# A hybrid decoder layer on one core: one head's attention put behind the next head's K/V quad, an operand block in another slot, two row vectors sent through DRAM, and the meta products raised in rank

## The chip, the core and the metric

The kernel runs on one core of a Trainium2 chip. Its time is the device time of one execution, in microseconds, from the first instruction to the last and what little lies around them; a comparison is made between medians of several runs. The engines are PE (matmuls, with its own weight loads, PEld), DVE (elementwise work and reductions), ACT (copies, casts, activations), POOL (elementwise work) and SP, which here only issues DMAs. Each engine works through its own list of instructions in order and waits on semaphores for the others.

## What is computed

One layer over 2048 tokens of width 1024, with 16 learned meta tokens ahead of them:

```python
hn = rms_norm(h, norm_g)                        # h = meta tokens, then x
proj = hn @ w_in                                # 1024 x 4096
cx, cb, cc, cg, q, k, v, rg = split(proj, 8)    # 512 columns each
conv_out = cb * conv3(cc * cx) * silu(cg)       # causal, three taps
qf, kf = rotary(q) * 128 ** -0.5, rotary(k)     # 4 heads of 128
ret = head_group_norm(retention(qf, kf, v)) * silu(rg)
y = rms_norm(h + concat(conv_out, ret) @ w_out, final_g)   # tokens of x alone
```

`retention` works in chunks of 128 tokens: inside a chunk the masked and decayed scores q k^T times v; across chunks a 128x128 state per head, which decays from chunk to chunk and takes up k^T v. The meta tokens give the first state and the first two columns of the convolution's history. All of it is in float32.

## The kernel before

**Products.** Every float32 operand of a large product is cast to a high part on ACT (L99, L102), and the rest is taken as a low part by a subtraction on DVE (L100, which calls L111, or L103). A product of two such operands is three matmuls: low x high, high x low, high x high. The work is cut in *quads*: a 2x2 arrangement of weight blocks (128 columns each, K over 4 tiles of 128) times a 2x2 arrangement of moving blocks (512 tokens each). `quad` (L199) does a quad as seven block products instead of eight, with sums and differences of the blocks as operands: 7 products x 4 K tiles x 3 matmuls = 84 matmuls of 128x512 at L208, product 0 to product 6, each against one moving operand m[0] to m[6]. The weights' sums are made on POOL and split by `stationary` (L121), in a ring of three buffers (RING); the moving operands stay in SBUF for a whole round, each high and low part in a slot of its own (`operand`, L139). `quad_plain` (L247) does a quad in eight block products, 96 matmuls at L258, and needs only the plain blocks: m[0], m[1], m[5] and m[7]. m[7] is the block B12, which no seven-product quad uses; it has no slot of its own and lies in slot 4 (`B12`, L33). The plain quads are done first in a round, while the operands that are sums get ready.

**Rounds.** The tokens are done in two rounds of 1024, and the output projection follows as a third stage. In a round come four heads (for each a K/V quad and a Q/RG quad), then four groups of the convolution (two quads each). In round 0 both quads of head 0 are plain; in round 1 and in the output stage only the first quad is. The four sums of round 1 and of the output's weights are made ahead by `prepare` (L181) while an earlier round runs, stored in DRAM (`sums_x`, `sums_w`), and read back by `prepared` (L191) into buffers t of the ring `gen` (GEN = 16 buffers, which also holds x, w, k, v, q, gates and outputs). SUMS (L34) says which operand each stored sum is: sum 0 is m[3], sum 1 is m[2], sum 2 is m[4], sum 3 is m[6]. At the turns of the rounds sums 1 and 3 are split before the plain quad and sums 0 and 2 after it. Slot 3 holds the plain weights (PLAIN_W) until the plain quad is done.

**Attention.** `head` (L517) traces the K/V quad, the Q/RG quad, the loads of the next quad's weights (`ahead`, L713), and then its attention: transposes of k and v (L573, L578), state updates (L588 on PE, L591 on DVE), scores (L601), the masked scores pm (L603, DVE), scores times v and q times state (L611, L612), group norm (L617 to L628), a transpose back (L635), the gate (L636) and a store.

**Row factors.** The factor 1/rms of every token is needed along the free axis. For each 512 tokens `row_factors` (L340) loads x, squares and sums on ACT (L317), takes the power on POOL (L274) and spreads the 512 values over all partitions with `spread` (L277): a diagonal matrix on DVE (L281), a matmul with ones on PE (L288), a copy and a square on ACT (L291, L293). Those of round 0 come early in round 0, those of round 1 in its convolution groups.

**Meta products.** In round 0 `meta_products` (L386) multiplies the 16 meta tokens with each of the quad's four raw weight blocks (L392): 4 K tiles x 4 blocks, two instructions each, so 32 small matmuls a call and eight calls.

**The order of the work.** `schedule_with_timeline_sim=True` (L825): a planner walks through the program before the run and fixes the order of each engine's list. It simulates the engines with its own estimates of durations, and whenever an engine is free it gives it, of the instructions that are ready in its simulation, the one of best rank. The rank is the place in program order; inside `tc.high_priority(offset=n)` an instruction ranks as if it stood n places earlier.

Of the kernel before, what the change touches and what calls it, by code (L numbers as in the profile page):

```python
# [32 lines left out]
FIRST_W, PLAIN_W, B12 = 2, 3, 4  # L33
# [35 lines left out]
def hybrid_trunk(ctx: ExitStack, tc: tile.TileContext, t, out: bass.AP, chunk_decay):  # L69
# [75 lines left out]
    def parts(m, i, kt, src, factor=None):  # L145
        hi, lo = operand(i, kt)
# [172 lines left out]
    def spread_factors(ss, rr, rr2):  # L319
# [5 lines left out]
        spread(rc, P, rr, rr2)  # L325
# [14 lines left out]
    def row_factors(r, f):  # L340

        f.extend([row_tile("rr"), row_tile("rr2"), []])
        for j in range(2):
            ss = small.tile([P, 2, CH], F32, name="ss", tag="ss")
            for c in range(CH):
                row_squares(ss, r, j, c)
                yield
            f[2].append(spread_factors(ss, *(a[:, j * HB : (j + 1) * HB] for a in f[:2])))
        yield
# [36 lines left out]
    def meta_products(blocks):  # L386
# [3 lines left out]
        for kt in range(KH):  # L390
            for i in (3, 2, 1, 0):
                nc.tensor.matmul(  # L392
                    four[i], meta_s[:, i % 2 * KH + kt, :], blocks[i][:, kt * P : (kt + 1) * P],
                    start=kt == 0, stop=kt == KH - 1,
                )
# [121 lines left out]
    def head(h, r, m, rot_t, f, blocks, ahead, first=(), between=()):  # L517


        between = iter(between)  # L520
# [19 lines left out]
        next(between, lambda: None)()  # L540
        q, sg = [None, None], [None, None]
# [25 lines left out]
        blocks = ahead()  # L567
        states = [state[h]]
# [73 lines left out]
        return blocks  # L642

    def output(pair, m, final_g):
# [78 lines left out]
    for r in range(NR):  # L723
# [7 lines left out]
        if r == 0:  # L731
# [3 lines left out]
            def begin(half):  # L735
# [4 lines left out]
                load_x(r), gain_of, {(0, 0): lambda: begin(0), (0, KH - 1): lambda: begin(1), (0, KT - 1): normalise_meta}  # L740
# [26 lines left out]
        else:  # L767
# [61 lines left out]
```

## Time and profile before

| | |
|---|---|
| median of 3 runs | 900.6 us (899.18 to 901.88) |
| the profiled execution | 903.85 us, of which its span is 902.1 |
| matmuls at L208, three groups of 1008 | mean 390 to 397 ns each |
| matmuls at L258, three groups of 128 | mean 395 to 396 ns each |
| DVE, split of a weight (L111 wl<-ra) x216 | mean 892 ns |
| ACT, cast of a weight (L99) x216 | mean 620 ns |
| POOL, weight sums (L111 ra<-ra) x72 | mean 1570 ns |
| HBM | 90.92 MB read, 25.17 MB written |

A row of a timeline reads: start in us from the span's start, length in us, engine, line, operation, out<-in, sizes, and in brackets how long the engine had stood idle before it and which instruction ended that. Matmuls overlap each other, so the pace of PE is read from the starts, not from the lengths. L12 is line 12 of the kernel before. A row of waits reads: who, for whom, us in total, times, longest.

### The profile page before, as it was taken

The page shows a single profiled execution, that of the slowest core. Times are in us where ns is not written, and L with a number is a line of the kernel's source. Part 1 is how long each engine was busy: PE and PEld are TensorE (multiplying, and loading weights), DVE is VectorE, ACT ScalarE, POOL GpSimd, SP SyncE. Part 2 cuts the span into 40 slices and gives each one's busy share as a digit, 9 for nine tenths or more (in the row PEclk, how much of TensorE's full clock was granted, in tenths as well). Part 3 has the DMA queues.
Part 4 walks back from the last instruction along what each step waited for, and adds up shares of the span by engine and source line. Part 5 has one row for each costly group of instructions (what it writes and reads, how often), then busy time and mean ns, then how long its engine had stood idle before and what let it go on. Part 6 is the DMA issues. An engine that isn't in the chain of part 4 may idle for free.

```text
span 902.1 us, 12862 instructions
## 1 busy us (share of the span) xinstructions
PE 885.0 (98%) x4407; PEld 727.8 (81%) x4407; DVE 714.6 (79%) x1173; ACT 406.1 (45%) x815; POOL 398.9 (44%) x294
## 2 busy tenths in 40 slices
PE   8998999999999999999999999999999999999996
PEld 5787888888878777788888888888888878788885
DVE  6798888897686776899889899777667697866764
ACT  8771342424344443655333332433333465554553
POOL 0533132323355554461333323345546445777763
PEclk9998999999999999999999999999999999999999
DMA  9711352623234232744125262113231685555532
GB/s 333 239 40 38 104 195 59 205 82 107 79 103 127 78 108 78 253 180 141 38 73 203 73 236 68 50 56 90 57 88 48 210 280 178 162 186 152 182 111 93
DMA packets 76242, 116.94 MB, mean 130 GB/s; under 512 B 7632, under 2 KB 24336, under 8 KB 76176
## 3 DMA queue, kind: packets, MB, share of 16 engines
q1 hardware_dynamic: 76176, 116.11, 40.1%
q8 instruction: 35, 0.57, 0.3%
q14 instruction: 31, 0.25, 0.1%
HBM read 90.92 MB, written 25.17 MB: 129 GB/s over the span
## 4 chain that ended last, share of the span: by engine, by line
PE 83%; DVE 9%; DMA 3%; ACT 2%; issue 2%; POOL 1%; SPq 0%; POOLq 0%; DVEq 0%; ACTq 0%
PE pj L208 66%; PE pj L258 7%; DVE ml L111 2%; DVE wl L111 2%; PE ms L611 2%; PE ms L612 1%; PE ms L601 1%; PE ms L588 1%; PE ms L392 1%; DVE rot L513 1%; DMA ra<-in_w_in 1%; PE ms L635 1%; PE ms L573 1%; DVE rot L512 1%; PE ms L578 1%
## 5 line engine op out<-in xcount | busy, mean ns | idle before, releaser
L208 PE MATMUL pj<-mh,wl 128*128 128x512 f32 x1008 | 400.0, 397 | 1.0 <-ACT tc L215 0.8
L208 PE MATMUL pj<-ml,wh 128*128 128x512 f32 x1008 | 394.2, 391 | 1.1 <-DVE ml L111 1.1
L208 PE MATMUL pj<-mh,wh 128*128 128x512 f32 x1008 | 393.4, 390 | 0.0
L99 ACT CAST wh<-ra 128x512 fp32r<-128x512 f32 x216 | 133.8, 620 | 315.1 <-PE pj L208 272.4
L208 PEld LDWEIGHTS pj<-mh,wl 128*128 128x128 f32 x1008 | 189.6, 188 | 43.1 <-ACT tc L215 2.2
L208 PEld LDWEIGHTS pj<-ml,wh 128*128 128x128 f32 x1008 | 189.8, 188 | 39.6 <-DVE ml L111 1.9
L208 PEld LDWEIGHTS pj<-mh,wh 128*128 128x128 f32 x1008 | 189.6, 188 | 39.8
L111 DVE TENSOR_TENSOR wl<-ra,wh 128x512 fp32r<-128x512 f32 x216 | 192.4, 892 | 36.2 <-ACT wh L99 35.2
L111 POOL TENSOR_TENSOR ra<-ra 128x512 f32<-128x512 f32 x72 | 113.0, 1570 | 82.0 <-DVE qg L556 32.3
L108 POOL TENSOR_TENSOR sa<-ra 128x512 f32<-128x512 f32 x36 | 54.9, 1525 | 122.6 <-DVE wl L111 62.1
L111 POOL TENSOR_TENSOR ra<-sa,ra 128x512 f32<-128x512 f32 x36 | 52.2, 1450 | 98.3 <-DVE wl L111 98.0
L215 ACT COPY tc<-pj 128x512 f32<-128x512 f32 x108 | 62.6, 580 | 0.0
L258 PE MATMUL pj<-ml,mh 128*128 128x512 f32 x128 | 50.8, 396 | 0.1
L258 PE MATMUL pj<-mh,mh 128*128 128x512 f32 x128 | 50.2, 395 | 0.0
L258 PE MATMUL pj<-mh,ml 128*128 128x512 f32 x128 | 48.5, 396 | 1.5 <-DVE ml L111 1.5
L624 POOL TENSOR_TENSOR rp<-rs,neg_half 128x4 f32<-128x4 f32 x16 | 19.9, 1245 | 51.0 <-DVE rs L108 50.8
L466 POOL TENSOR_TENSOR c<-c,rr 128x512 f32<-128x512 f32 x16 | 30.0, 1874 | 24.0 <-DVE c L454 13.6
L108 DVE TENSOR_TENSOR tc<-pj,tc 128x512 f32<-128x512 f32 x32 | 22.0, 688 | 23.4 <-PE pj L208 23.4
L111 DVE TENSOR_TENSOR ml<-t,mh 128x512 fp32r<-128x512 f32 x40 | 36.6, 961 | 0.8 <-ACT mh L99 0.8
L99 ACT CAST wh<-sa 128x512 fp32r<-128x512 f32 x36 | 22.3, 620 | 32.7 <-PE pj L208 32.7
L665 DVE TENSOR_TENSOR yo<-pj,yo 128x512 f32<-128x512 f32 x32 | 22.0, 688 | 18.8 <-POOL yo L108 8.9
L466 POOL TENSOR_TENSOR c<-c,tc 128x512 f32<-128x512 f32 x16 | 27.3, 1706 | 19.0 <-ACT tc L492 17.6
(128 smaller groups left out, 1134.3 us busy)
## 6 DMA issues: line engine op xcount, KB each, us to landing
ra<-in_w_in SPq DMA_DIRECT2D x128, 256.0 KB, 2.7
x<-in_xT SPq DMA_DIRECT2D x48, 256.0 KB, 5.1
w<-in_w_out SPq DMA_DIRECT2D x32, 256.0 KB, 5.0
ra<-mixed SPq DMA_DIRECT2D x32, 256.0 KB, 2.7
yo<-in_x SPq DMA_DIRECT2D x32, 256.0 KB, 4.4
ra<-in_x SPq DMA_DIRECT2D x16, 256.0 KB, 3.7
mixed<-qg SPq DMA_DIRECT2D x16, 256.0 KB, 2.3
sums_x<-x SPq DMA_DIRECT2D x16, 256.0 KB, 2.4
```

Source lines behind the costliest of these rows:

```text
L99: nc.scalar.copy(out=hi, in_=src)
L108: eng.tensor_tensor(out=out, in0=a, in1=b, op=ALU.add)
L111: eng.tensor_tensor(out=out, in0=a, in1=b, op=ALU.subtract)
L208: nc.tensor.matmul(bank, a[:, ks], b, start=first and kt == 0 and n == 0, stop=kt == KH - 1 and n == 2, skip_group_check=not first,)
L215: nc.scalar.copy(out=c, in_=bank)
L258: nc.tensor.matmul(banks[i], a[:, ks], b, start=half + kt + n == 0, stop=half == 1 and kt == KH - 1 and n == 2,)
L392: nc.tensor.matmul(four[i], meta_s[:, i % 2 * KH + kt, :], blocks[i][:, kt * P : (kt + 1) * P], start=kt == 0, stop=kt == KH - 1,)
L466: eng.tensor_tensor(out=out, in0=a, in1=b, op=ALU.mult)
L512: nc.vector.tensor_tensor(out=rot[:h, :w], in0=a[h:], in1=table[h:, 1, :], op=ALU.mult)
L611: nc.tensor.matmul(o[:, cs], pm[:, cs], vt[j][:, cs], start=True, stop=False)
L624: nc.gpsimd.tensor_tensor(out=rp, in0=rs, in1=neg_half.rearrange("p (c a) -> p c a", a=1), op=ALU.pow)
L665: last[0] = nc.vector.tensor_tensor(out=y, in0=pp, in1=y, op=ALU.add)
```

## The change

Four edits. (1) `head` becomes a generator of three parts: K/V quad, Q/RG quad and loads, attention. In round 0 the attention of head 0 is traced after the K/V quad of head 1; all other heads keep their order. (2) B12 takes slot 4 only in round 0; in round 1 and the output stage it takes slot 6, so that sums 1 and 2 (m[2], m[4]) are split before the plain quad and sums 0 and 3 (m[3], m[6]) after it; sum 0 is loaded before it. (3) The row factors of round 1 are written to DRAM and read back with one row going to all partitions; the square is then taken from SBUF. (4) The matmuls of `meta_products` rank 400 places earlier (HIGH).

```diff
-FIRST_W, PLAIN_W, B12 = 2, 3, 4
+FIRST_W, PLAIN_W = 2, 3
...
-    def operand(i, kt):
-        slot = B12 if i == 7 else i
+    def operand(i, kt, slot=None):
+        slot = i if slot is None else slot
...
-    def moving(load, scale=None, after={}):
+    def moving(load, scale=None, after={}, spare=6):
...
-                    parts(m, BLOCK[half][j], kt, blocks[-1], scale(k) if scale else None)
+                    i = BLOCK[half][j]
+                    parts(m, i, kt, blocks[-1], scale(k) if scale else None, spare if i == 7 else i)
...
-    def prepared(m, src, ns):
-
+    def load_sums(src, ns):
+
+        tiles = []
         for n in ns:
             for kt in range(KH):
                 a = gen("t")[:, :HB]
                 nc.sync.dma_start(a, src[n, kt])
-                parts(m, SUMS[n], kt, a)
+                tiles.append((SUMS[n], kt, a))
+        return tiles
+
+    def prepared(m, src):
+
+        for i, kt, a in load_sums(src, (1, 2)):
+            parts(m, i, kt, a)
+        rest = load_sums(src, (0,))
+
+        def finish():
+            for i, kt, a in rest + load_sums(src, (3,)):
+                parts(m, i, kt, a)
+
+        return finish
...
-        spread(rc, P, rr, rr2)
+        if row is None:
+            spread(rc, P, rr, rr2)
+        else:
+            nc.sync.dma_start(row.rearrange("(c p) -> p c", c=CH), rc)
+            nc.sync.dma_start(rr, row.partition_broadcast(P))
+            nc.scalar.activation(rr2, rr, AF.Square)
...
+            row = dram.tile([HB], F32, name="row", tag=f"row{j}") if r else None
+            f[2].append(spread_factors(ss, *(a[:, j * HB : (j + 1) * HB] for a in f[:2]), row))
...
+        with tc.high_priority(offset=HIGH):
+            for kt in range(KH):
+                for i in (3, 2, 1, 0):
+                    nc.tensor.matmul(
...
         next(between, lambda: None)()
+        yield
         q, sg = [None, None], [None, None]
...
         blocks = ahead()
+        yield blocks
         states = [state[h]]
...
             w = plain_parts(loads)
-            prepared(m, sums_w, (1, 3))
+            finish = prepared(m, sums_w)
             quad_plain(w, m, take)
-            prepared(m, sums_w, (0, 2))
+            finish()
...
-            prepared(m, sums_x, (1, 3))
-            between = (lambda: prepared(m, sums_x, (0, 2)),)
+            between = (prepared(m, sums_x),)
...
+        attend = None
         for h in range(NG):
-            blocks = head(h, r, m, rot_t, f, blocks, lambda: ahead(r, h + 1), *((first, between) if h == 0 else ()))
+            steps = head(h, r, m, rot_t, f, blocks, lambda: ahead(r, h + 1), *((first, between) if h == 0 else ()))
+            next(steps)
+            if attend:
+                next(attend, None)
+            blocks, attend = next(steps), steps
+            if r + h > 0:
+                next(attend, None)
+                attend = None
```

In round 0 `moving` is called with `spare=4`.

More of the change, by code (lines that the diff above doesn't have):

```diff
@@ L143, in operand, with parts @@
         return hi, lo
-    def parts(m, i, kt, src, factor=None):
-        hi, lo = operand(i, kt)
+    def parts(m, i, kt, src, factor=None, slot=None):
+        hi, lo = operand(i, kt, slot)
         split(hi, lo, src, factor)
         m[i].append((hi, lo))
-    def moving(load, scale=None, after={}):
+    def moving(load, scale=None, after={}, spare=6):
         m = [[] for _ in range(8)]
@@ L317, in row_squares, with spread_factors @@
             nc.scalar.activation(a, a, AF.Square, accum_out=ss[:, half, c : c + 1])
-    def spread_factors(ss, rr, rr2):
+    def spread_factors(ss, rr, rr2, row=None):
         add(nc.vector, ss[:, 0, :], ss[:, 0, :], ss[:, 1, :])
@@ L389, in meta_products @@
         four = [bank[i * 32 : i * 32 + NMETA, :P] for i in range(4)]
[L390 to L395, printed above, removed]
+        with tc.high_priority(offset=HIGH):
+            for kt in range(KH):
+                for i in (3, 2, 1, 0):
+                    nc.tensor.matmul(
+                        four[i], meta_s[:, i % 2 * KH + kt, :], blocks[i][:, kt * P : (kt + 1) * P],
+                        start=kt == 0, stop=kt == KH - 1,
+                    )
         scratch = sb.tile([P, HB], F32, name="mk", tag="tc", bufs=COPIES).rearrange("p (a c) -> p a c", a=CH)
@@ L641, in head @@
             nc.gpsimd.tensor_copy(out=state[h], in_=states[-1])
-        return blocks
     def output(pair, m, final_g):
@@ L739, in hybrid_trunk @@
             m, b = moving(
-                load_x(r), gain_of, {(0, 0): lambda: begin(0), (0, KH - 1): lambda: begin(1), (0, KT - 1): normalise_meta}
+                load_x(r), gain_of, spare=4, after={(0, 0): lambda: begin(0), (0, KH - 1): lambda: begin(1), (0, KT - 1): normalise_meta}
             )
```

1 line of the change is left out of this document (removed).

## The prediction

> **What bounds the kernel now.** I read the page first, then the waits of PE, then the PE and DVE timelines around each wait, and last the windows of the slice in which the granted clock falls.
>
> ```profile
> PE 885.0 (98%) x4407; PEld 727.8 (81%) x4407; DVE 714.6 (79%) x1173; ACT 406.1 (45%) x815; POOL 398.9 (44%) x294
> ```
>
> PE is busy for 98% of the span, so only two things can shorten the run: matmul time that goes away, or the few places where PE stands still. The waits of PE name the latter.
>
> ```profile
> PE ms L611 <- DVE pm L603: 3.7, 1, 3.7
> ...
> PE pj L208 <- ACT tc L215: 0.8, 2, 0.7
> ```
>
> The longest is one wait of 3.7 us, in the attention of head 0 in round 0, for the masked scores pm. The PE timeline shows it, and what follows it; below it stand the same stretch of head 1, a calm stretch, and two windows.
>
> ```profile
> 75.67 0.39 PE L208 MATMUL pj<-mh,wh 128*128 128x512 f32 x1
> ...
> 83.24 0.77 PE L208 MATMUL pj<-mh,wl 128*128 128x512 f32 x1
> ...
> 85.77 0.40 PE L208 MATMUL pj<-mh,wl 128*128 128x512 f32 x1
> ```
>
> ```profile
> 132.61 0.39 PE L208 MATMUL pj<-mh,wh 128*128 128x512 f32 x1
> ...
> 134.68 0.48 PE L208 MATMUL pj<-mh,wl 128*128 128x512 f32 x1
> ```
>
> ```profile
> 768.18 0.39 PE L208 MATMUL pj<-mh,wh 128*128 128x512 f32 x1
> ...
> 769.54 0.39 PE L208 MATMUL pj<-mh,wh 128*128 128x512 f32 x1
> ```
>
> ```profile
> 71.68:78.70 7.02, 4.38 (x25) 3.48 (x23) 6.89 (x13) 1.72 (x3) 1.20 (x1) 1.00 0.18 53
> 78.72:85.55 6.83, 5.74 (x22) 5.26 (x23) 4.56 (x17) 0.00 (x0) 2.04 (x3) 0.50 0.10 38
> ```
>
> In a window row the columns are PE, PEld, DVE, ACT and POOL busy, then the granted clock. For head 0 the step from the last product matmul over the eight score-times-value and state matmul pairs to the next product matmul takes 83.24 - 75.67 = 7.57 us; for head 1 it takes 134.68 - 132.61 = 2.07. That is 5.5 us of excess, part wait, part half clock: for 6.83 us the granted clock is 0.50. The half clock also stretches the next products: six starts from 83.24 to 85.77 take 2.53 us. In the calm stretch six steps take 769.54 - 768.18 = 1.36, or 0.227 each, so another 1.1 is lost. **The stall and its clock dip cost 6.6 us together.**
>
> The Trainium skill, "TensorE: Matmul & The Clock Gate", Part 1, says that the clock is halved after an idle window of about 3.4 us and comes back after a busy one. The dip of 6.83 us right after a 3.7 us wait agrees. By this rule a wait that is cut in two shorter ones has no dip.
>
> Why pm is late is in the DVE timeline (and one POOL row of the same time).
>
> ```profile
> 58.23 1.68 DVE L513 TENSOR_TENSOR rot<-kv,rot_t 64x512 f32<-64x512 f32 x1
> 59.95 3.37 DVE L111 TENSOR_TENSOR ml<-t,mh 128x512 fp32r<-128x512 f32 x2
> ...
> 64.85 0.67 DVE L111 TENSOR_TENSOR wl<-ra,wh 128x512 fp32r<-128x512 f32 x1
> ...
> 75.27 0.69 DVE L111 TENSOR_TENSOR wl<-ra,wh 128x512 fp32r<-128x512 f32 x1
> ...
> 76.68 0.68 DVE L513 TENSOR_TENSOR rot<-kv,rot_t 64x512 f32<-64x512 f32 x1
> ...
> 79.01 0.74 DVE L603 SCALAR_TENSOR_TENSOR pm<-ms,cols,causal 128x512 f32<-128x512 f32 x1
> ```
>
> ```profile
> 59.45 1.62 POOL L111 TENSOR_TENSOR ra<-sa,ra 128x512 f32<-128x512 f32 x1
> ```
>
> DVE is busy for 6.89 of the 7.02 us before the dip: it works off a backlog of splits and rotations, and pm stands in its queue behind them, among others the K rotation of head 1. In this stretch DVE sets the pace, not PE.
>
> **The change part by part.** *Head 0's attention after the next K/V quad.* Nothing is added or removed; in program order, which ranks the work for the planner that fixes every engine's order, head 0's transposes, scores and pm now follow the 84 matmuls (19 us) of head 1's K/V quad. Upper end: pm no longer has to be ready at 75.67, the wait and its dip go, 6.6 us. Lower end: the backlog itself does not shrink, so another PE instruction may meet it. Without attention matmuls in between, the K/V quad reaches products sooner than DVE splits their weights.
>
> ```profile
> 58.31 0.48 PE L208 MATMUL pj<-mh,wl 128*128 128x512 f32 x1
> ```
>
> Product 0 starts here. Product 2, 24 matmuls on, would be due at 58.31 + 24 x 0.227 = 63.8, its low part is ready at 64.85 + 0.67 = 65.5: a wait of 1.7. Product 5 would then be due 36 matmuls later at 73.7; its low part is ready at 75.27 + 0.69 = 76.0, a wait of 2.3, or less by the state updates that DVE no longer does before it. Together about 3.8, in two pieces, each shorter than the 3.7 that the dip followed; so no dip, and 6.6 - 3.8 = 2.8 us are left as gain. Between 2.8 and 6.6 I take 4.8: the planner puts attention matmuls that are ready into waits that it foresees, so part of the 3.8 is filled. The kv and qg tiles of two heads now live together, 4 x 4 = 16, all of GEN; as the older head is served first I cost that at nothing, and a take that waits for a tile if it fails.
>
> *Meta products whole.* Eight calls of 32 matmuls stand in sixteen groups in the PE timeline; the first is whole, the last is a rest of four.
>
> ```profile
> 34.80 0.39 PE L258 MATMUL pj<-ml,mh 128*128 128x512 f32 x1
> 35.12 1.07 PE L392 MATMUL ms<-ra,meta_s 128*16 128x128 f32 x32
> ...
> 36.45 0.40 PE L258 MATMUL pj<-mh,ml 128*128 128x512 f32 x1
> ```
>
> ```profile
> 337.85 0.39 PE L208 MATMUL pj<-mh,wh 128*128 128x512 f32 x1
> 338.16 0.83 PE L392 MATMUL ms<-ra,meta_s 128*16 128x128 f32 x18
> 338.92 0.50 PE L208 MATMUL pj<-mh,wl 128*128 128x512 f32 x1
> 339.26 0.39 PE L208 MATMUL pj<-ml,wh 128*128 128x512 f32 x1
> ...
> 341.87 0.40 PE L392 MATMUL ms<-ra,meta_s 128*16 128x128 f32 x4
> 342.20 1.13 PE L288 MATMUL ms<-rot,ones 128*128 128x512 f32 x2
> ...
> 343.39 0.39 PE L208 MATMUL pj<-ml,wh 128*128 128x512 f32 x1
> ```
>
> From the product matmul before a group to the second one after it, less two steps of 0.227: the whole group costs 36.45 - 34.80 - 0.45 = 1.20, the 18 of the last call 339.26 - 337.85 - 0.45 = 0.96. So 14 matmuls more cost 0.24, and a visit costs some 0.6 before it does any work. Eight visits go. About four stand alone, 0.5 each (a little under the 0.6, as the line through two points is rough): 2.0. The other four touch another small group (a meta state, a transpose, a spread) and share its entry and exit; I give them 0.1 each, 0.4 in all. Sum 2.4; ends 1.2 (two visits at 0.6, the rest cut anew) and 4.8 (all eight at 0.6). Earlier issue makes no one wait: the weights are loaded anyway, ACT's four copies stay at their old rank.
>
> *Row factors of round 1 through DRAM.* Two spreads of row factors over the partitions go: the DVE diagonal, the PE matmul pair, the ACT copy out of PSUM. On PE one costs 343.39 - 342.20 = 1.19 less the 339.26 - 338.92 = 0.34 with which any return from a small group begins: 0.85, twice 1.7. Ends 1.5 and 1.8. Added are two DMAs each on SP and a square on ACT that was there before.
>
> ```profile
> final_g<-in_final_g SPq DMA_DIRECT2D x1, 512.0 KB, 4.7
> ...
> sums_w<-w SPq DMA_DIRECT2D x16, 256.0 KB, 2.1
> ```
>
> ```profile
> 294.17 4.68 SPq L431 DMA_DIRECT2D ra<-in_w_in  x3
> ```
>
> ```profile
> 427.86 0.69 DVE L556 TENSOR_TENSOR qg<-qg,rr 128x512 f32<-128x512 f32 x1
> ```
>
> No row shows a store of 4-byte pieces; the nearest are a store of 2.1 and the broadcast load of final_g of 4.7, 7 us in all, and three times that would still do: the second spread stands at 342.20, the factors are first used at 427.86. Behind the store in SP's queue stand the next weight loads (the row at 294.17, three issues spread over 4.68 us as buffers come free); they feed a quad ahead, so I cost a delay of a few us at nothing. If that cover were gone, PE would lose the 2 to 7 us once or twice.
>
> *B12 in another slot.* At the two turns sums 1 and 2 are split before the plain quads, 0 and 3 after; sum 0 is loaded early. In round 1 PE has no wait after its plain quad, so nothing is won there. At the output turn it has one.
>
> ```profile
> 772.69 0.50 PE L208 MATMUL pj<-ml,wh 128*128 128x512 f32 x1 [0.71 <-DVE ml L111]
> 773.03 0.39 PE L208 MATMUL pj<-mh,wh 128*128 128x512 f32 x1
> ```
>
> ```profile
> 758.38 1.37 DVE L665 TENSOR_TENSOR yo<-pj,yo 128x512 f32<-128x512 f32 x2 [3.44 <-PE pj L258]
> ...
> 769.18 4.66 DVE L111 TENSOR_TENSOR ml<-t,mh 128x512 fp32r<-128x512 f32 x4
> ```
>
> From 769.54, the last row of the calm stretch, to 773.03 six steps take 3.49 instead of 1.36: 2.1 us lost, because product 4 needs operand 4 (sum 2), whose four splits begin only at 769.18. They now come before the plain quad; operand 6, which takes their place, is needed two products later, and the load of sum 0 is early enough to use DVE's idle 3.44 us at 755. I take 2.1; ends 0 and 2.5 (a later ACT wait of 0.4 may go too). The 0.8 of waits for ACT copies may go or stay: taken as nothing. A new order of every queue may also cost some tenths: 0.4 off.
>
> Sum: 4.8 + 2.4 + 1.7 + 2.1 - 0.4 = 10.6. The profiled execution took 903.85, of which 902.1 is its span, so its like would take 893.3; the median of the three runs, 900.6, lies 3.3 below it, and 900.6 - 10.6 = 890.0 is my number.
>
> **The rivals.** *The backlog moves on.* DVE operations that take 0.68 alone (76.68) take 1.68 beside POOL (58.23), and the change moves neither POOL's work nor the splits. Then PE meets the same lateness at head 1's products: gain 2.8 instead of 4.8, 892.0; if it meets it in one piece, with the dip, nothing is won there: 894.8. For it: DVE is full until 79. Against: ready attention matmuls can fill the waits. The Trainium skill, "SBUF — State Buffer", section "SBUF: two separate sides", has this as a rule: a DVE instruction with two SBUF inputs and a GpSimd one that reads SBUF exclude each other. The 1.68 agrees, and by it the backlog stays.
>
> *B12 comes too late.* This one ends slower. Slot 6 is free only when the last product of the last quad is done; then B12 must be split before the second half of the plain quad.
>
> ```profile
> 740.96 0.39 PE L258 MATMUL pj<-mh,mh 128*128 128x512 f32 x1
> ```
>
> ```profile
> 741.43 1.78 DVE L111 TENSOR_TENSOR ml<-w,mh 128x512 fp32r<-128x512 f32 x1
> ```
>
> The last product ends at 740.96 and 31 of 48 plain matmuls are left: B12 is due 31 x 0.227 = 7.0 us later. Four splits at 1.78 are 7.1, and the first two suffice to go on. But if the planner puts the eight splits of sums before them (eight at 0.7 to 1.2, some 7.5 us), PE waits 7.5 at each turn, with a dip of up to 2.9 each (the 6.6 less the 3.7 of waiting): 20.8 us against the 8.5 won elsewhere, 912.9. It decides from waits above 8.5 in sum. Against it: B12 precedes the sums in program order.
>
> *It does not do what it says.* If urgent meta products are cut again because their loads land one by one, 2.4 goes: 892.4.
>
> **How the numbers follow.** Forecast 0.62; the backlog moves 0.22 (892 to 895); meta still cut 0.06; nothing left but small parts, about even, 0.05; B12 too late 0.05. Range: the upper ends together, 6.6 + 4.8 + 1.8 + 2.5 = 15.7, give 885; the lower ones, 2.8 + 1.2 + 1.5 + 0 - 0.4 = 5.1, give 895.5; with a bit of the case of 894.8 I say 885 to 896. A difference under 0.3%, 2.7 us, can't be told from none. Faster 0.91, same 0.05, slower 0.04.
>
> **What would show it.** Right: no PE wait over 1 us for pm, PEclk without the dip in the fourth slice, eight L392 groups of 32, L288 only in round 0, no wait near 770 after the output's plain quad. Wrong: a wait of L208 on wl between 60 and 80 us; a wait of L258 on ml some 10 us into a plain quad; SP's loads late after the row store.

## The result and the profile after

The change makes the kernel slower: 927.2 us median (925.04 to 930.12, 6 runs) against 902.13 (899.18 to 904.76, 6 runs), a ratio of 1.0282 with a 95% interval of 1.0254 to 1.031. I had forecast 890. The profiled execution took 926.49 us, its span 924.7, so 22.6 us more than the span before.

In the kernel after, line numbers have moved: the matmuls of `quad` are L224 (before L208), those of `quad_plain` L274 (L258), the meta products L416 (L392), pm L630 (L603); the casts and splits L99, L102, L103 and L111 have kept theirs. Page of the kernel after, with the busy time of each engine and the granted clock in 40 slices, and one row of its list of DMA issues:

```profile
PE 887.0 (96%) x4403; PEld 731.9 (79%) x4403; DVE 707.6 (77%) x1171; ACT 406.5 (44%) x813; POOL 398.6 (43%) x294
...
PEclk9999999999999898998999999999999999899999
...
row<-rc SPq DMA_DIRECT2D x2, 2.0 KB, 9.8
```

PE's share has fallen from 98% to 96%. The dip (a stretch at half clock) in the fourth slice is gone, as forecast, but four slices (14, 16, 19 and 35) show one now, each of 6.83 us. The last row is the new store: 2 KB take 9.8 us to land.

The waits of PE in the kernel after:

```profile
PE pj L224 <- DVE wl L111: 16.7, 5, 6.1
PE pj L224 <- ACT wh L99: 3.0, 1, 3.0
...
PE pj L224 <- DVE kv L108: 1.6, 1, 1.6
PE pj L274 <- DVE ml L103: 1.5, 1, 1.5
PE pj L274 <- DVE c L490: 1.3, 1, 1.3
```

The old first entry, 3.7 us for pm, is down to 1.3, and in its place PE waits 16.7 us for low parts of weights. Where, is best seen by setting the start of the k-th product matmul after against the k-th before (both from the PE timelines, counted from 0, 3408 of them in both):

| product matmul | 252 | 336 | 420 | 1008 | 1092 | 1176 | 1260 | 1344 | 1596 | 2688 | 2940 | last |
|---|---|---|---|---|---|---|---|---|---|---|---|---|
| after less before, us | -7.8 | -5.6 | +0.7 | -1.1 | +7.4 | +5.8 | +13.5 | +13.5 | +19.7 | +19.8 | +22.8 | +22.8 |

Four things are lost: the early lead of 7.8 us (up to 420), two steps of 8.4 and 7.7 us in round 0's convolution groups, 6.2 at round 1's turn (1344 to 1596) and 3.0 at the output turn. The PE timeline of the kernel after has a wait at each place; the number in brackets is the idle time:

```profile
65.42 0.47 PE L224 MATMUL pj<-mh,wl 128*128 128x512 f32 x1 [1.80 <-DVE wl L111]
80.06 0.50 PE L224 MATMUL pj<-mh,wl 128*128 128x512 f32 x1 [1.64 <-DVE kv L108]
...
123.46 0.50 PE L224 MATMUL pj<-mh,wl 128*128 128x512 f32 x1 [2.74 <-DVE wl L111]
...
312.50 0.80 PE L224 MATMUL pj<-mh,wl 128*128 128x512 f32 x1 [6.06 <-DVE wl L111]
360.44 0.79 PE L224 MATMUL pj<-mh,wl 128*128 128x512 f32 x1 [5.84 <-DVE wl L111]
414.63 0.50 PE L274 MATMUL pj<-ml,mh 128*128 128x512 f32 x1 [1.49 <-DVE ml L103]
416.92 0.80 PE L274 MATMUL pj<-mh,ml 128*128 128x512 f32 x1 [1.33 <-DVE c L490]
792.21 0.77 PE L224 MATMUL pj<-mh,wl 128*128 128x512 f32 x1 [2.99 <-ACT wh L99]
```

A first matmul of 0.77 to 0.80 us instead of 0.50 shows the half clock. The ACT timeline of the kernel after shows why the waits at 312 and 360 are there (the second looks the same):

```profile
298.93 1.07 ACT L422 COPY mk<-ms 16x128 f32<-16x128 f32 x4
310.59 0.63 ACT L347 ACTIVATE rr<-rr 128x512 f32<-128x512 f32 x1 [10.58 <-DMA rr<-row]
311.12 1.12 ACT L99 CAST wh<-ra 128x512 fp32r<-128x512 f32 x2
```

ACT stands for 10.58 us at the square of the row factors, because they are still under way, and the casts of the next weights stand behind it. But SP, too, held its next weight loads (ra) for 9.4 us behind the store, so the trace alone does not say which of the two queues held PE:

```profile
295.73 0.38 SPq L345 DMA_DIRECT2D row<-rc  x1
305.17 0.33 SPq L346 DMA_DIRECT2D rr<-row  x1
305.59 0.86 SPq L455 DMA_DIRECT2D ra<-in_w_in  x2
```

All three signs that the prediction had named for being wrong are there: the wait of 1.80 us on wl at 65, the one of 1.49 on ml in round 1's plain quad, and SP's late loads.

### The profile page after: what moved, and what is told of

The parts are those of the page before. It is cut to its first block, busy times and chain, and to the rows that moved or that the text cites. A ratio compares the mean times of both kernels' runs of the same rounds, so it can differ in the third digit from the quotient of the medians.

```text
span 924.7 us, 12862 instructions
## 1 busy us (share of the span) xinstructions
PE 887.0 (96%) x4403; PEld 731.9 (79%) x4403; DVE 707.6 (77%) x1171; ACT 406.5 (44%) x813; POOL 398.6 (43%) x294
## 4 chain that ended last, share of the span: by engine, by line
PE 51%; DVE 10%; DMA 6%; issue 3%; ACT 2%; POOL 2%; SPq 0%; POOLq 0%; DVEq 0%; ACTq 0%
PE pj L224 45%; DVE ml L111 2%; DVE wl L111 2%; DMA row<-rc 2%; PE pj L274 2%; DMA n<-in_x 1%; DMA rr<-row 1%; ACT wh L99 1%; DMA ra<-in_w_in 1%; ACT mh L99 1%; ACT mh L102 1%; PE ms L615 1%; DVE w L111 1%; PE ms L639 1%; PE ms L628 1%
## 5 line engine op out<-in xcount | busy, mean ns | idle before, releaser
L224 PE MATMUL pj<-mh,wl 128*128 128x512 f32 x1008 | 402.0, 399 | 22.3 <-DVE wl L111 16.7
L224 PE MATMUL pj<-ml,wh 128*128 128x512 f32 x1008 | 396.2, 393 | 0.0
L224 PE MATMUL pj<-mh,wh 128*128 128x512 f32 x1008 | 396.1, 393 | 0.0
L99 ACT CAST wh<-ra 128x512 fp32r<-128x512 f32 x216 | 133.8, 621 | 325.0 <-PE pj L224 282.8
L111 DVE TENSOR_TENSOR wl<-ra,wh 128x512 fp32r<-128x512 f32 x216 | 194.6, 903 | 65.6 <-ACT wh L99 65.2
L224 PEld LDWEIGHTS pj<-mh,wl 128*128 128x128 f32 x1008 | 191.3, 190 | 65.1 <-DVE wl L111 16.3
L224 PEld LDWEIGHTS pj<-mh,wh 128*128 128x128 f32 x1008 | 191.0, 189 | 40.1
L224 PEld LDWEIGHTS pj<-ml,wh 128*128 128x128 f32 x1008 | 191.5, 190 | 38.1
L111 POOL TENSOR_TENSOR ra<-ra 128x512 f32<-128x512 f32 x72 | 111.6, 1550 | 62.0 <-issue 24.1
L108 POOL TENSOR_TENSOR sa<-ra 128x512 f32<-128x512 f32 x36 | 54.3, 1509 | 133.5 <-DVE wl L111 47.0
L111 POOL TENSOR_TENSOR ra<-sa,ra 128x512 f32<-128x512 f32 x36 | 51.3, 1424 | 126.6 <-DVE wl L111 118.7
L274 PE MATMUL pj<-ml,mh 128*128 128x512 f32 x128 | 52.0, 406 | 1.5 <-DVE ml L103 1.5
L274 PE MATMUL pj<-mh,mh 128*128 128x512 f32 x128 | 51.6, 403 | 0.0
L274 PE MATMUL pj<-mh,ml 128*128 128x512 f32 x128 | 49.2, 404 | 1.7 <-DVE c L490 1.3
L108 POOL TENSOR_TENSOR yo<-yo,tc 128x512 f32<-128x512 f32 x21 | 33.4, 1593 | 9.2 <-ACT tc L231 9.2
L99 ACT CAST wh<-sa 128x512 fp32r<-128x512 f32 x36 | 22.4, 622 | 32.8 <-PE pj L224 32.6
L111 DVE TENSOR_TENSOR ml<-t,mh 128x512 fp32r<-128x512 f32 x40 | 35.6, 925 | 1.3 <-ACT mh L99 1.2
L108 DVE TENSOR_TENSOR tc<-pj,tc 128x512 f32<-128x512 f32 x32 | 22.0, 686 | 17.8 <-PE pj L224 17.7
```

The costliest lines, as they stand in the source:

```text
L99: nc.scalar.copy(out=hi, in_=src)
L108: eng.tensor_tensor(out=out, in0=a, in1=b, op=ALU.add)
L111: eng.tensor_tensor(out=out, in0=a, in1=b, op=ALU.subtract)
L224: nc.tensor.matmul(bank, a[:, ks], b, start=first and kt == 0 and n == 0, stop=kt == KH - 1 and n == 2, skip_group_check=not first,)
L274: nc.tensor.matmul(banks[i], a[:, ks], b, start=half + kt + n == 0, stop=half == 1 and kt == KH - 1 and n == 2,)
```

## The experiments

All are compared with the kernel before on the same chip. The line numbers of `quad` are L224 or L214 in them, by what each contains.

### Each edit alone

**Head 0's attention deferred** (edit 1 alone):

```diff
+            next(steps)
+            if attend:
+                next(attend, None)
+            blocks, attend = next(steps), steps
```

> The kernel before with the first edit alone: head 0's attention in round 0 follows head 1's K/V quad. Theory of the prediction: 4.8 us faster (2.8 to 6.6). Theory of crowding, from the changed kernel's trace: the two waits of the first K/V quad go and their clock dip with them (6 to 8 us ahead by head 1's first product), but the same DVE work then stands ahead of the next quads' weight splits, with waits of 1.3 to 2.7 us on wl of L111 and pm in heads 1 and 2, so that by the end of head 2 nothing of it is left: within 2 us of before. If it is within 2 us, crowding; if 3 us or more are gained and stay until the end, the prediction's price was right and another edit spoils it.

Measured: 904.16 us against 902.71, ratio 1.0013 (1.0002 to 1.0024), 1.5 us slower. The theory of crowding fits, not the price that I had set.

**B12 in slot 6** (edit 2 alone):

```diff
+    def moving(load, scale=None, after={}, spare=6):
...
+        for i, kt, a in load_sums(src, (1, 2)):
+            parts(m, i, kt, a)
+        rest = load_sums(src, (0,))
```

> The kernel before with the second edit alone: B12 in slot 6 at the two turns and the other sums loaded in the new order. Theory of the prediction: 2.1 us faster, all of it at the output turn. Theory of the late last sum, from the changed kernel's trace: 6.2 us lost at round 1's turn (two waits of 1.5 and 1.3 us, on ml of L103 and on c of L490, and a clock dip of 6.83 us) and 3.0 us at the output turn (a wait of 3.0 us on wh of L99 and a dip), in all 9 us slower. The first theory needs the PE waits ahead of the output's first product to go with no other in their place; the second needs the two dips in this run.

Measured: 910.04 us against 902.71, ratio 1.0081 (1.0061 to 1.0101). At round 1's turn 6.7 us are lost in the profiled run, with a dip; at the output turn 0.9, a wait of 2.96 in place of the old ones. Smaller than expected by the share at the output turn.

**Row factors through DRAM** (edit 3 alone):

```diff
+            nc.sync.dma_start(row.rearrange("(c p) -> p c", c=CH), rc)
+            nc.sync.dma_start(rr, row.partition_broadcast(P))
+            nc.scalar.activation(rr2, rr, AF.Square)
```

> The kernel before with the third edit alone: round 1's row factors go through DRAM. Theory of the prediction: 1.7 us faster, the length of the 16 spread products taken off PE, with both transfers hidden. Theory of the held queue, from the changed kernel's trace: twice a wait of some 6 us for the weight split behind the round trip, each with a clock dip of 6.83 us that costs 3.4 us of PE time, less 1.7 us: 16 us slower in two steps of 8.

Measured: 915.69 us against 902.71, ratio 1.0142 (1.012 to 1.0164): 13 us slower, in two steps of 7.3 and 7.5.

**Meta products whole** (edit 4 alone):

```diff
+        with tc.high_priority(offset=HIGH):
```

> The kernel before with the fourth edit alone: each head's 32 meta products stand in one group. Both theories have it faster: the prediction by 2.4 us (1.2 to 4.8), the reading of the two traces by 2 to 3 us, as what is left when the other three edits' shares (0, 9 and 16 us slower) are taken from the difference of 25 us. If it is slower, the shares of the other three are wrong.

Measured: 900.68 us against 902.71, ratio 0.998 (0.9968 to 0.9991), 2.0 us faster. All its eight groups have 32 matmuls.

The four add to +1.5 + 7.3 + 13.0 - 2.0 = 19.8 us; together they cost 25.1. In the profiled runs, where the gap is 7.8 us, 4.2 of it arise in the output stage: edits 3 and 4 alone gain 1.1 each there, edit 2 alone loses 0.9, the whole loses 3.0. The 1.1 is the same in both, a wait of 1.17 us at 731.53 in the output's plain quad of the kernel before, and it can go only once. The wait of 2.96 us that edit 2 alone has at the output turn has no dip, the one of 2.99 in the whole kernel has one ("The half clock" below says why). The rest of the gap I have not followed.

### What holds PE behind the row factors

**ACT's squares held back**, SP's queue unchanged: the squares get a bias of zero that is made from round 1's last x tile.

```diff
-            nc.scalar.activation(rr2, rr, AF.Square)
...
+            zero = small.tile([P, 1], F32, name="zero", tag="zero")
+            nc.vector.tensor_scalar(out=zero, in0=b[-1][:, :1], scalar1=0.0, scalar2=0.0, op0=ALU.mult, op1=ALU.add)
+            for j in range(2):
+                js = slice(j * HB, (j + 1) * HB)
+                nc.scalar.activation(f[1][:, js], f[0][:, js], AF.Square, bias=zero)
```

> The third edit alone, but ACT's two squares of the row factors are held back to round 1 (their bias is a zero made from round 1's last x tile); SP's queue is as in the third edit alone, which took 915.7 us against 902.7. Theory A, the square holds ACT: in the third edit alone ACT waits 10.2 us for rr ahead of the weight casts, and that makes the two waits of PE on wl. With the squares late both waits and both dips go, and the time is 902.7 - 1.7 = 901, at most 903. Theory S, SP's queue holds the weight loads behind the load of rr: the two PE waits of about 5 us and the dips stay, 914 to 916. Between, if either alone would hold PE by 2 to 3 us: 906 to 910.

Measured: 900.23 against 902.86, ratio 0.997 (0.9955 to 0.9985). Its store is as slow as in the third edit alone and SP waits for it as it did there (8.7 us from the store to the load, by its timeline); its list of DMA issues says:

```profile
rr<-row SPq DMA_DIRECT2D x2, 256.0 KB, 4.8
...
row<-rc SPq DMA_DIRECT2D x2, 2.0 KB, 9.4
```

No PE wait between 290 and 370 is left. Theory A holds.

**Both DMAs on POOL's queue**, the square in its place:

```diff
-            nc.sync.dma_start(row.rearrange("(c p) -> p c", c=CH), rc)
-            nc.sync.dma_start(rr, row.partition_broadcast(P))
+            nc.gpsimd.dma_start(row.rearrange("(c p) -> p c", c=CH), rc)
+            nc.gpsimd.dma_start(rr, row.partition_broadcast(P))
```

> The third edit alone, but both DMAs of a round trip are issued from POOL, so that SP's queue holds nothing back; ACT's square stays where it was, behind the load. Theory A (ACT's wait): both PE waits on wl stay, 913 to 916 us. Theory S (SP's queue): they go, 901 to 903. By either one POOL itself waits for the store ahead of its next operations, which could add a wait of its own.

Measured: 914.58 us against 902.86, ratio 1.0126 (1.011 to 1.0143). SP is free and 11.7 of the 13.0 us are lost all the same, behind PE waits of 3.94 and 3.45 us on wl. ACT timeline of this run:

```profile
311.08 0.63 ACT L337 ACTIVATE rr<-rr 128x512 f32<-128x512 f32 x1 [9.95 <-DMA rr<-row]
```

ACT stands at the same square as in the kernel after. With the run before it this settles the cause: ACT's list, which is worked through in order.

**Pieces of 16 bytes** (the factors stand permuted in the row, so round 1's are not the reference's):

```diff
-            nc.sync.dma_start(row.rearrange("(c p) -> p c", c=CH), rc)
+            nc.sync.dma_start(row.rearrange("(p c) -> p c", c=CH), rc)
```

> The third edit alone, but the store writes the four factors of a partition side by side: 128 pieces of 16 bytes instead of 512 of 4. The factors then stand permuted in the row, so round 1's factors are not the reference's; the amount of work is the same. If the landing time goes with the number of pieces, the store takes 9.5/4 = 2.4 to 4 us instead of 9.5, ACT's wait falls from 10.2 to 3 to 5 us, and the time to 903 to 907. If it is a fixed cost of a store that is waited for, it stays at 8 to 9.5 and the time at 914 to 916.

Measured: 902.44 us against 902.86, ratio 0.9994 (0.9981 to 1.0006). List of DMA issues of this run:

```profile
rr<-row SPq DMA_DIRECT2D x2, 256.0 KB, 3.9
...
row<-rc SPq DMA_DIRECT2D x2, 2.0 KB, 2.2
```

The same 2 KB land in 2.2 us. ACT still waits 3.83 and 2.63 us for rr, and no product matmul between 290 and 370 waits for a weight. The Trainium skill, "DMA: Bandwidth & Descriptors", section "Rules for kernel authors", says that a last dimension which isn't contiguous becomes one descriptor per element; the fall from 9.5 to 2.2 with a quarter of the pieces agrees in direction.

### What makes the slot late

**The second edit with B12 back in slot 4**; the sums are loaded in the new manner, in the order that slot 4 asks for.

```diff
-    def moving(load, scale=None, after={}, spare=6):
+    def moving(load, scale=None, after={}, spare=4):
...
-        for i, kt, a in load_sums(src, (1, 2)):
+        for i, kt, a in load_sums(src, (1, 3)):
...
-            for i, kt, a in rest + load_sums(src, (3,)):
+            for i, kt, a in rest + load_sums(src, (2,)):
```

> The second edit alone, with B12 back in slot 4: the sums are still loaded in the second edit's manner (two split before the plain quad, one loaded early, the fourth at the end), but sums 1 and 3 come first, 0 is loaded early and 2 is last, as slot 4 demands. Theory of the late slot: slot 6 is read until the last product of the quad before, so the planner puts the sums' splits ahead of B12's and the last three x splits come at 402.6 us, after PE wants them. With slot 4 the x splits stand ahead of the sums again and the loss of 5.7 us at round 1's turn is gone: 902 to 904 in all, the output turn as before. Theory of the early loads: the extra early load and the new order of the sums on SP, ACT and DVE hold the splits back, whatever the slot; then 4 to 6 us stay lost at round 1's turn: 906 to 910.

Measured: 903.32 against 902.7, ratio 1.0008 (0.9999 to 1.0017). Nothing is lost at round 1's turn. DVE timelines, first of the second edit alone, then of this run (L103 is a split of an x block, L111 ml<-t of a sum, L111 wl of a weight):

```profile
394.44 1.28 DVE L111 TENSOR_TENSOR ml<-t,mh 128x512 fp32r<-128x512 f32 x2
395.65 1.78 DVE L111 TENSOR_TENSOR wl<-ra,wh 128x512 fp32r<-128x512 f32 x1
397.35 0.68 DVE L111 TENSOR_TENSOR ml<-t,mh 128x512 fp32r<-128x512 f32 x1
397.95 1.76 DVE L111 TENSOR_TENSOR wl<-ra,wh 128x512 fp32r<-128x512 f32 x1
399.63 0.74 DVE L103 SCALAR_TENSOR_TENSOR ml<-x,gain,mh 128x512 fp32r<-128x512 f32 x1
400.30 1.76 DVE L111 TENSOR_TENSOR ml<-t,mh 128x512 fp32r<-128x512 f32 x1
401.98 0.68 DVE L490 TENSOR_TENSOR c<-pj,c 128x512 f32<-128x512 f32 x1
402.58 2.06 DVE L103 SCALAR_TENSOR_TENSOR ml<-x,gain,mh 128x512 fp32r<-128x512 f32 x3
```

```profile
392.50 1.78 DVE L103 SCALAR_TENSOR_TENSOR ml<-x,gain,mh 128x512 fp32r<-128x512 f32 x1
394.20 0.68 DVE L111 TENSOR_TENSOR ml<-t,mh 128x512 fp32r<-128x512 f32 x1
394.81 0.74 DVE L103 SCALAR_TENSOR_TENSOR ml<-x,gain,mh 128x512 fp32r<-128x512 f32 x1
395.47 0.68 DVE L490 TENSOR_TENSOR tc<-tc,rr 128x512 f32<-128x512 f32 x1
396.07 1.89 DVE L111 TENSOR_TENSOR ml<-t,mh 128x512 fp32r<-128x512 f32 x3
```

With slot 6 the last three x splits come at 402.58, behind sums and weights that are needed later; with slot 4 the last one is done at 395.5. The wait at the output turn stays: 3.02 us for a weight cast, and 2.2 us are lost there, this time with a dip of 3.41 us. As the sums stand in the old order here and one of them is only loaded earlier, that wait comes with the new manner of loading them, not with the slot.

### Where the gain of the deferred attention goes

**The preparation after head 2:**

```diff
-            if h > 0:
+            if h > 1 - r:
                 next(later, None)
                 next(later, None)
```

> The first edit alone, with one more change: in round 0 the preparation of round 1's sums (L174's subtractions on DVE and their loads and stores) starts after head 2 instead of after head 1. The first edit alone is 8.05 us ahead of before at the 253rd product and 5.85 at the 337th, and loses it all up to the 421st, with waits of PE at 117 to 123 us on kv and wl while DVE does L174. Theory of the collision: without L174 there these waits go and 4 to 6 us stay won at the 421st product; if the preparation then fits beside heads 2 and 3, the time is 897 to 899. Theory of the full DVE: the backlog of splits moves on in any case, the waits come at 117 to 123 or later in the same sum, and the time stays at 902 to 905.

Measured: 904.64, ratio 1.0016 (1.0006 to 1.0025). DVE now has 18.1 us of work from 100 to 124 instead of 22.2, and PE still has waits of 1.64 and 1.19 us that end at 119.39 and 122.61. So a collision with the preparation is not enough.

**Head 2's meta products from other data**, with the preparation late and with it in its place:

```diff
-        return blocks, meta_products(blocks) if r == 0 else None
+        return blocks, meta_products(blocks if n != 2 else [rot_t[:, 0, :HB]] * 4) if r == 0 else None
```

> The first edit alone with the preparation after head 2, as in the run before, and head 2's meta products read the position tables instead of head 2's weights, so that the meta state of head 2 is another one; the number of products is the same. With the preparation late, DVE stood idle for 3.2 us at 113 and PE still waited for 1.8 and 1.4 us at 117 to 121, behind a chain: PE's meta products of head 2 (114.6 to 116.7), POOL's in-place sums of the same weights (116.85 on), ACT's casts, DVE's low parts (121.86). Theory of the chain: with POOL freed from the meta products its sums come before 114, the two waits go, and 3 to 5 us are won at the 421st product, 899 to 901 in the end. Theory of the full DVE: the waits stay in the same place or come back later in the same sum, 903 to 905.

> As the run before it in this list, but with the preparation after head 1, as the first edit has it. It tells whether the preparation's work on DVE alone is enough to hold PE: if the chain from the meta products to POOL's sums was the only cause, this run gains as much as the other (899 to 901); if both hold PE, as the trace of the first edit alone has it (DVE is busy for 22.2 of the 24 us from 100 to 124), this one stays at 902 to 905 while the other gains; if neither, both stay.

Measured: 904.87 (1.0012 to 1.003) and 905.43 (1.0018 to 1.0047), both against 902.7. In the first the waits at 117 to 123 are gone, and others come one head later: 1.64, 1.22 and 0.44 us, at 168 to 176. In the second the same two of 1.64 and 1.22 us come there, at 169 to 175. So neither theory stood as I had put it: freeing the weights moves the loss but does not lift it. And in the first run head 2's meta products still stood at 114.46 although their data had long been there. What they share with the attention is the ring of four PSUM banks (tag "ms"), which I take to be handed out in program order; the deferral puts twelve banks of head 0's attention shortly ahead of them.

**The meta products from head 2 on take a bank of the product ring** (tag "pj"), with the first edit and without it:

```diff
-    def meta_products(blocks):
+    def meta_products(blocks, take_bank=ps_misc):
 
-        bank = ps_misc()
+        bank = take_bank()
...
-        return blocks, meta_products(blocks) if r == 0 else None
+        return blocks, meta_products(blocks, ps_proj if n >= 2 else ps_misc) if r == 0 else None
```

> The first edit alone, and from head 2 on the meta products take their PSUM bank from the ring of the four product banks instead of the ring of four that the attention uses. In the built order head 2's meta products then stand at products 324 to 360 instead of 384, so POOL can begin head 2's sums 20 to 60 products sooner. Theory of the bank: the waits at 117 to 121 us go and do not come back in head 3; 3.5 to 5 us of the 5.85 that PE was ahead at the 337th product stay, 898 to 900. Theory of the full weight chain (POOL, ACT and DVE can't prepare weights faster, whatever the order): the waits come back in another place in the same sum, 903 to 905.

> The kernel before with that change of bank alone. Before, PE has no wait for weights between 85 and 380 us, so both theories have nothing to gain here: 901.5 to 904. If it gains as much as the run before it, the bank and not the deferral is what is worth something; if it is slower by 1 us or more, the borrowed product bank costs that in itself and the run before has to be read against this one.

Measured: 901.4 with the deferral (0.9968 to 0.9992), 904.77 without (1.0003 to 1.0026), both against 903.07. So with this bank the deferral is worth 3.4 us, with the old one it cost 1.5. The first meta row for head 2 in the PE timelines, first edit alone and then with the other bank:

```profile
114.74 1.06 PE L406 MATMUL ms<-ra,meta_s 128*16 128x128 f32 x30
...
119.00 0.49 PE L605 MATMUL ms<-kv,kd 128*128 128x128 f32 x2 [1.38 <-ACT kv L599]
```

```profile
97.87 0.84 PE L406 MATMUL pj<-ra,meta_s 128*16 128x128 f32 x22
...
110.76 0.41 PE L406 MATMUL pj<-ra,meta_s 128*16 128x128 f32 x8
```

POOL sums the weights in place, so it can begin only when the meta products have read them: 115.94 in the one run, 111.31 in the other. The waits at 117 to 124 are gone and do not come back. That the old ring of banks held the meta products is what this pair of runs shows; without the deferral the same change of bank wins nothing.

### The parts that gain, together

**Edit 4, and edit 3 with the squares held back** (edits 1 and 2 are left out):

```diff
+        with tc.high_priority(offset=HIGH):
...
+            nc.sync.dma_start(rr, row.partition_broadcast(P))
...
+                nc.scalar.activation(f[1][:, js], f[0][:, js], AF.Square, bias=zero)
```

> The two parts that are left with a gain: the fourth edit and the third with ACT's squares held back to round 1; the first and second edits are left out. Alone they gave -2.0 and -2.7 us. Part of both was the same early stretch (a clock dip of 3.41 us in place of 6.83), so they add to 3.5 to 4.7 us: 898 to 899.3. If the extra priority of the meta products delays the weight chain again, 900 to 901.

Measured: 898.91 against 902.7, ratio 0.9954 (0.994 to 0.9968).

**The same with the other bank**, first with edit 1 and then without it:

```diff
+        return blocks, meta_products(blocks, ps_proj if n >= 2 else ps_misc) if r == 0 else None
```

> The first, third and fourth edits together, mended: ACT's squares held back, the meta products from head 2 on in a product bank; the second edit is left out. Theory of the bank: the 3.5 to 5 us of the deferral come on top of the 3.8 of the two other edits, less the early dip, which all of them share: 894 to 897. Theory of the full weight chain: 899 to 902, no better than 898.9 without the deferral.

> The same without the deferral: third edit with the squares held back, fourth edit, the meta products from head 2 on in a product bank. Both theories: as the run with the two edits and the old bank, 898.9, within 1 us.

Measured: 894.41 (0.9877 to 0.992) and 896.46 (0.9901 to 0.9946), both against 903.07. The first is 1% faster than the kernel before and the best version here. The intervals overlap and the two profiled spans are 893.0 and 893.1 us, so it is not settled whether the deferral adds anything on top. The other bank was worth more than the 1 us I allowed it in the second; why is open. Page and waits of the first:

```profile
PE 876.2 (98%) x4403; PEld 725.7 (81%) x4403; DVE 711.5 (80%) x1172; ACT 408.4 (46%) x813; POOL 402.3 (45%) x294
...
PEclk9999999999999999999999999999999999999999
```

```profile
PE pj L214 <- DVE wl L111: 2.1, 2, 1.6
PE pj L214 <- DVE kv L108: 1.7, 1, 1.7
```

No dip is left that shows in a slice (one of 3.41 us stands at 8.46, during the first loads). The longest waits inside the quads are two in head 1's K/V quad, in products 2 and 6.

## Why the prediction was wrong

By the single runs the deferral cost 1.5 us where I had summed a gain of 4.8, the slot cost 7.3 (forecast: a gain of 2.1), the row factors cost 13.0 (a gain of 1.7), and the meta products gained 2.0 (2.4).

**The row factors: the step that failed most.** I costed "a square on ACT that was there before" at nothing. It was there, but it used to wait for PSUM and now waits for the trip through DRAM, and ACT's list is in order, so the casts of the next weights wait with it: 10.58 us. I had asked only for the DMAs what is queued behind them, and took the cover of 85 us up to the first multiplication for the cover of everything. The length of the trip was not the mistake: 9.8 + 4.8 = 14.6 us is twice the estimate and within the allowance. The two steps of 8.4 and 7.7 us are waits of 6.06 and 5.84 and the half clock that comes with each. "PE would lose the 2 to 7 us once or twice" was near the loss at its upper end, but by ACT's list and not by SP's. With the squares held back, the edit gives 2.6 us (1.4 to 4.1) where I had said 1.7; in its profiled run 1.8 of it are won between products 504 and 1180, where the two spreads stood.

**B12: the rival came true at one turn.** "In round 1 PE has no wait after its plain quad, so nothing is won there" left out that something can be lost. The step that failed is the order that I took from the program: the rival had the mechanism, slot 6 free only after the last product and the sums' splits put ahead, and got 0.05, because "B12 precedes the sums in program order". Rank decides only among instructions that are ready: while slot 6 is still read, B12 is not, and DVE's list gets the sums instead. I priced it at 7.5 us of wait a turn plus a dip of 2.9; it took 6.2 at round 1's turn. At the output turn the waits that I had read at 769 to 773 did go, and another took their place. DVE and ACT timelines of the kernel after:

```profile
784.01 5.19 DVE L111 TENSOR_TENSOR ml<-t,mh 128x512 fp32r<-128x512 f32 x3
789.12 0.68 DVE L691 TENSOR_TENSOR yo<-pj,yo 128x512 f32<-128x512 f32 x1
```

```profile
789.89 0.63 ACT L693 ACTIVATE rot<-yo 128x512 f32<-128x512 f32 x1 [4.38 <-DVE yo L691]
...
790.52 0.60 ACT L99 CAST wh<-ra 128x512 fp32r<-128x512 f32 x1
```

The splits that now come earlier take 1.73 us each, and behind them stands the output addition, behind that an ACT square, behind that the weight cast that PE waits for. I had counted the splits at their place, and put what they push back at nothing.

**Head 0's attention: one wait right, one elsewhere, the third missed.** The wait for pm and its dip went. Product 2 of the next K/V quad waits 1.80 us for its low part where I had worked out 1.7. The wait of 2.3 for product 5's low part did not come; in its place product 6 waits 1.64 us until DVE has read its bank (L108, kv). So the sum of the two was about right, partly by luck. But the lead of 7.8 us was not all gain. From product 205 to product 504 the first edit alone has waits of 1.80 + 1.65 + 1.38 + 2.33 = 7.2 us where the kernel before has one of 3.75 and its dip, 6.6 together; and by product 336 it had done 165 small matmuls where the kernel before had done 185, so part of the lead was postponed work. The last two are the missing ones, and they are gone when head 2's meta products take a bank of another ring; I had only counted the SBUF tiles that two heads share (16 of 16), not the PSUM banks. The rival "The backlog moves on" foresaw that little would be left, at worst nothing; alone the edit costs 1.5 us. Its cause, a DVE that can't keep up, did not hold: with another bank the deferral wins 3.4 us against the same kernel without it.

**Meta products whole: right in kind, small in size.** 2.4 forecast, 2.0 measured (0.8 to 2.9). Sixteen groups became eight, as forecast. But in the profiled run of this edit 1.3 us are won by product 1344, near my lower end, and the other 1.1 is the wait in the output's plain quad, which I had not named. That the number came out so close is partly luck.

**The half clock.** In the first heads the kernel after has two waits of 1.80 and 1.64 us and no dip; at round 1's turn it has two, of 1.49 and 1.33, and a dip. Windows of the kernel after (columns as in the prediction):

```profile
77.99:81.40 3.41, 1.77 (x8) 1.13 (x8) 3.41 (x9) 0.62 (x1) 0.45 (x1) 1.00 0.34 77
...
412.49:415.90 3.41, 1.61 (x6) 0.68 (x5) 3.41 (x3) 1.59 (x3) 2.54 (x2) 1.00 0.14 45
415.90:422.73 6.83, 5.81 (x14) 4.56 (x15) 6.75 (x11) 0.00 (x0) 0.00 (x0) 0.50 0.24 81
...
787.97:791.38 3.41, 1.25 (x6) 0.71 (x4) 3.41 (x4) 1.49 (x4) 2.18 (x2) 1.00 0.02 8
```

The longest single wait there is 1.49 us, yet the clock halves for 6.83 us after 3.41 us of which PE was busy for 1.61. The Trainium skill, "TensorE: Matmul & The Clock Gate", Part 1, speaks of an idle window of about 3.4 us. I had made of it that "a wait that is cut in two shorter ones has no dip", and the turn shows that this does not hold: a stretch need not be idle throughout.

Where a wait lies decides as well. The dips of the kernel after begin at 310.10, 357.88, 415.91 and 791.38, which are 14, 17 and 110 times 3.413 us apart, so the stretches that count seem to lie on a fixed grid. On that grid the wait of 2.99 us at the output turn lies mostly in the stretch before 791.38, which leaves PE busy for 1.25 us, and a dip follows. The wait of 2.96 us of edit 2 alone lies across a border of its own grid (its dip at 402.04 plus 110 times 3.413 gives 777.5), and none follows:

```profile
774.09:777.50 3.41, 1.76 (x8) 1.13 (x6) 3.41 (x5) 1.01 (x3) 2.18 (x2) 1.00 0.10 37
777.50:780.92 3.42, 2.11 (x9) 1.79 (x10) 3.42 (x3) 1.70 (x4) 3.26 (x3) 1.00 0.29 77
```

Likewise the wait of 1.80 us at 65 lies across a border, and the one of 1.64 us leaves PE busy for 1.77 in its stretch (77.99:81.40). Whether a wait of 1.5 to 3 us costs a dip is thus in part luck of its place. A sharp bound does not show: in the run with pieces of 16 bytes 1.65 us busy (74.13:77.54) had no dip behind it, in the one with the bank alone 2.08 us busy (770.78:774.19) had one of 3.41 us.

## What to carry to other kernels

When a transfer takes the place of an on-chip step, list every instruction that reads its result, and for each what stands behind it in its engine's list: cover is only as long as the time to the first of them. When a buffer, a slot or a bank is shared by other work, ask when its last reader is done and what a planner will put in front of the instruction that waits for it. A lead measured halfway is a gain only if the same work has been done by then.

## What the hardware showed beyond that

- A store of 2 KB in 512 pieces of 4 bytes lands in 9.4 to 9.8 us (10.4 from POOL's queue), in 128 pieces of 16 bytes in 2.2.
- A half clock of 6.83 us can follow a stretch of 3.41 us in which PE was busy for 47%, with no single wait over 1.5 us. The dips of one run begin whole multiples of 3.413 us apart, and nearly the same wait at the same place had a dip in one run (2.99 us) and none in another (2.96 us), by where it lay on that grid.
- ACT stood 10.58 us at an instruction that reads a DMA's result, and the casts behind it stood too; moving the DMAs to another queue left 11.7 of 13.0 us of the loss, moving the instruction removed it.
